# Attention scores in batches of four units instead of two, with the value products and output transposes of the loop in one PSUM bank

## The chip, the cores and the metric

The kernel runs on one core of a Trainium2 chip. The metric is the device time of one execution in microseconds (us). Of the kernel before there are three timed runs (median 454.51, from 453.69 to 454.97) and one profiled execution of 453.1 us, whose span from the first to the last instruction is 451.3 us.

## The reference

One encoder layer over 1024 tokens of width 1024. A combined projection makes queries, keys, values and gates of two groups of eight heads (head size 64). Group A attends within a window of 8 rows by 16 columns of the token grid (16 rows of 64) with a bias per head; group B attends within 128 tokens to either side, with two shared key/value heads, rotary positions and a sink logit. Both outputs are gated and concatenated, projected, added to the input and normalised:

```
h = x @ W_in
s = einsum('bqhd,biqjhd->bhqij', q_r, k_win) * scale + bias ; p = softmax(s)   # group A
s = where(valid, einsum('bnqkgd,bnjkd->bnkgqj', qb, k_band) * scale, -1e30)     # group B
p = softmax(concat([s, sink]))[..., :-1]
mixed = concat([y_a * silu(z_a), y_b * silu(z_b)])
x = layer_norm(alpha * x + mixed @ W_out, ln_gain, ln_bias)
```

## The kernel before, in words

Every product with a float32 operand is done as a sum of 16-bit ones: each operand is split into a high half and the rest, and high by high, high by rest and rest by high are added up in PSUM. For q times k the split halves of a query are stacked to 128 rows (64 of the high half, 64 of the rest): one product over 128 rows gives high by high plus rest by high at once (line 908), and a second one over 64 rows adds high by the rest of the key (line 912). The head `j` of a pair sets whether those 64 rows are the lower or the upper half of the array.

The work has four stages. Up to about 60 us: loading, scales and the value projection (lines 607 and 661). From 60 to 122 us: the first six column groups of the projection (line 404). From 122 to about 376 us: the attention loop, which also carries the other 15 column groups and the start of the output projection. After that: the rest of the output projection (line 1137) with the normalisation.

The attention loop has 128 units, each one head of one block of 128 queries; 64 of group B come first, then 64 of group A. A unit goes through these stages, each written at a fixed step `i` of the loop:

- `stage_mm` (lines 908 and 912) puts its scores into a PSUM bank of the tag `s`. Before, it is called at every even step for the units `i` and `i + 1`: two products over 128 rows, then two over 64 rows.
- `stage_qk` (line 937, VectorE): adds the bias or mask from the bank, writes `sn` and its minimum `nm`. Step `i`.
- `stage_exp` (line 952, ScalarE): the exponential of `sn`, written back into the unit's bank, with its sum. Step `i`.
- `stage_tr` (lines 962 on ScalarE, 963 on VectorE, 966 a transposing DMA of the SyncE queue): the high half and the rest of the probabilities, read from the bank, transposed into `tr`. Step `i + 1`. After line 963 the bank is free.
- `stage_pv` (line 992): for four units (a quad `q`) 30 or 36 small products of `tr` with the values, into a bank of the tag `t`. Step `4q + 9`.
- `stage_on` (line 1000, VectorE): divides by the sums. One step later.
- `stage_ot` (line 1010, four transposes, then line 1013 or 1019 on VectorE, which multiplies the gate `z`): before, for two quads at once, into another bank of the tag `t`, ahead of the value products of every second quad.

PSUM has eight banks of 128 x 512 float32: two for the projections (`pj`), four for scores (`s`) and two for all else (`t`), handed out in turn by `bank(tag)`; who takes a bank again waits for its last reader.

The order on each engine is the order in which the code is written. Between the stages `pump_to(u)` writes projection products ("fill") by a table: so many are due when the loop has reached step `u` (`FILL_N`, `FILL_AT`; 48 products for a column group, 24 to a half, about 24 for four units). The other engines' work for those groups is queued and taken out by `pop` at fixed places of a step. Once the loop has ended the order is that of the framework's scheduler (`final`).

Of the kernel before, what the change touches and what calls it, by code (L numbers as in the profile page):

```python
# [17 lines left out]
HD = 64  # L18
GW = 64
# [33 lines left out]
NPE = 384  # L53
PRE_AT = (12, 20)
WO_AT = [80, 84, 88, 92, 128, 129, 130, 131]
WO_LD = [18, 22, 26, 30, 36, 39, 42, 45, 48, 112, 116, 33, 130, 130]
# [10 lines left out]
def hybrid_block(ctx, tc, xT, x, wt, wv, wo, bias, sink, gain, lbias, cos, sin, bmask, out):  # L67
# [11 lines left out]
    def bank(tag):  # L79
        bufs = {"pj": 2, "s": 4, "t": 2}[tag]  # L80
        return (ps1 if bufs == 1 else ps2).tile([128, 512], F32, tag=tag, name=f"ps_{tag}", bufs=bufs)
# [162 lines left out]

    def w_scale(n):
# [190 lines left out]
    with ExitStack() as vctx:  # L436
# [139 lines left out]

        ROT = ("pj", "s", "t", "s")
        banks = {(t, a): bank(ROT[t]) for a in range(2) for t in range(4)}
        ordered.enter_context(tc.manual_schedule())
# [83 lines left out]

        set_a = [bank(r) for r in ROT]
        for i in range(3):
# [5 lines left out]
        for k in (0, 2):  # L671
            x2_lo(k)
        set_b = [bank(r) for r in ROT]
        for n, t in enumerate((2, 0, 1, 3)):
            for k in range(KT):
                for i in range(3):
                    v16(set_b[t], t, 1, k, i)
                if (n, k) == (0, 6):
                    w_scale(0)
                    w_split(0)  # L680
                    w_split(1)
                    x2_lo(4)
                    x2_lo(6)
                    x2_lo(7)
                if (n, k) == (1, 5):
                    w_scale(1)
# [44 lines left out]

        def z_sum(n):
            zps[n] = bank("t")
            nc.tensor.matmul(zps[n][:, :128], ones, cs[:, zabs[n] % 4], start=True, stop=True)
# [29 lines left out]
        def m_scale(i):  # L764
            n = NPRO + ZSUM[-1]
            if i == 0:
                z_sum(n)
# [205 lines left out]
    def stage_pv(q):  # L973
        ps = st[q, "o"] = bank("t")
        for m in range(4):
# [18 lines left out]
    def stage_on(q):  # L994
        ps = st.pop((q, "o"))
        ri = ap.tile([128, 4], F32, tag="ri", name="ri", bufs=4)
        nc.vector.reciprocal(ri, st.pop((q, "sm")))
        if q % 2 == 0:
            on[q // 2] = ap.tile([128, 2, 4, HD], F32, tag="on", name="on", bufs=2)
        nc.vector.tensor_mul(on[q // 2][:, q % 2], ps[:, :4 * HD].rearrange("p (m e) -> p m e", e=HD),  # L1000
                             ri.unsqueeze(2).to_broadcast([128, 4, HD]))

    def stage_ot(q):
        g, p, h = quad(q)
        h = h // 2
        need(*stk_ops.get(f"zb{p}" if g == "b" else f"z{p}", ()))
        ps = bank("t")
        o = on.pop(q // 2).rearrange("p q m e -> p (q m e)")
        for i in range(4):
            nc.tensor.transpose(ps[:, 128 * i:128 * i + 128], o[:, 128 * i:128 * i + 128], identf)  # L1010
        if g == "b":
            z = zt[4 + p][:, 512 * h:512 * h + 512]
            nc.vector.scalar_tensor_tensor(z, ps, z_col(4 + p), z, op0=ALU.mult, op1=ALU.mult)
        else:
            for i in range(2):
                b = 2 * h + i
                z = zt[p].rearrange("p (r c) -> p r c", c=GW)[:, :, 16 * b:16 * b + 16]
                src = ps[:, 256 * i:256 * i + 256].rearrange("p (r c) -> p r c", c=16)
                nc.vector.scalar_tensor_tensor(z, src, z_col(p), z, op0=ALU.mult, op1=ALU.mult)

# [33 lines left out]
    def wo_turn():  # L1054
        ps = bank("t")
        nc.tensor.transpose(ps[:, :128], wog.to_broadcast([128, 128]), identf)
# [97 lines left out]
    def final():  # L1154
# [96 lines left out]
        halves, normed = {}, [0]  # L1251
        for t, tag in ((0, "t"), (1, "t"), (2, "s")):
# [7 lines left out]
        tags = iter(("pj", "t", "pj", "t", "s", "s", "s", "s"))  # L1260
        for t, a in ((3, 1), (4, 1), (5, 0), (5, 1), (6, 0), (6, 1)):
# [18 lines left out]
    def gain_load():  # L1280
        gain_tile.append(zslot("gb"))
        nc.sync.dma_start(gain_tile[0], gain.partition_broadcast(128))

    clock["step"] = 0
    scan_ops = []
    for i in range(-LD, NU + LO):
# [33 lines left out]
        if i < NU:  # L1320
            if i % 2 == 0:
                us = units[i:i + 2]
                for u in us:
                    if u[3] in (0, 4):
                        need(*stk_ops[f"b{u[1]}", u[2], u[3] // 4])
                    if u[0] == "a" and i % 16 == 0:
                        need(*stk_ops[u[1], u[2], 0], *stk_ops[u[1], u[2], 1])
                stage_mm(us)
            stage_qk(units[i])
# [113 lines left out]
```

## Time and profile before

| | |
|---|---|
| three timed runs | 453.69, 454.51, 454.97 us |
| profiled execution, and its span | 453.1 us, 451.3 us |
| PE busy | 442.9 us (98%), 3271 products |
| weight loads (PEld) busy | 242.0 us (54%) |
| DVE (VectorE), ACT (ScalarE), POOL (GpSimd) busy | 344.9, 309.3, 219.0 us |
| line 404, projection products | 1008, 512 columns each |
| lines 908 and 912, score products | 128 each |
| TensorE clock granted | 0.997 of full speed |

A row of the timeline gives the start in us, the length in us, the engine, the line, the operation, `output<-inputs`, the shape and how many like instructions follow each other; in brackets the engine's idle time ahead of it and what ended it. Products overlap in the array, and the ends of products are modelled: how long one occupies the engine is read from the distance between two starts, not from its length. PEld is the load of the weights that stay in the array during a product. A row of a table by stretches gives start:end, the length, and for each engine its busy time and number of instructions, then the granted clock, the share of the DMA engines and GB/s.

### The profile page before, as it was taken

To read this page: it belongs to the slowest core of one execution; us is meant where nothing else is said; L and a number is where in the kernel's file an instruction comes from. 1 tells how busy PE (TensorE), PEld (TensorE's weight loads), DVE (VectorE), ACT (ScalarE), POOL (GpSimd) and SP (SyncE) were. 2 spreads that over 40 slices of the span, in tenths; PEclk is the share of its full clock that TensorE was granted. 3 is DMA by queue.
4 is the path that set the end of the run, shared out by engine and by line. 5 is a ranking of instruction groups with operands and counts; after the bars stand their busy time and mean duration, and the time that the engine had idled before them with its cause. 6 is when DMAs were issued, how large, how long until landed. Compare 5 with 4: busy or idle time off the path is not lost.

```text
span 451.3 us, 9483 instructions
## 1 busy us (share of the span) xinstructions
PE 442.9 (98%) x3271; PEld 242.0 (54%) x3271; DVE 344.9 (76%) x854; ACT 309.3 (69%) x718; POOL 219.0 (49%) x224
## 2 busy tenths in 40 slices
PE   9999999999999999999999999999999999999994
PEld 8996754444444455544545555555455554444442
DVE  5969958749988877777797888897776756379954
ACT  7679369767688988798978878887976876002211
POOL 0003934547838558658507528565662546005840
PEclk9999999999999999999999999999999999999998
DMA  8973088976847797597699799999999979101721
GB/s 297 378 254 93 14 284 260 303 275 241 253 130 155 130 191 143 124 147 158 130 176 200 166 166 195 198 223 175 204 209 178 168 139 371 52 0 62 248 87 70
DMA packets 133984, 81.76 MB, mean 181 GB/s; under 512 B 101296, under 2 KB 113328, under 8 KB 133680
## 3 DMA queue, kind: packets, MB, share of 16 engines
q1 hardware_dynamic: 133504, 80.67, 73.2%
q8 instruction: 25, 0.41, 0.4%
q10 hardware_dynamic: 432, 0.49, 0.3%
q14 instruction: 23, 0.19, 0.1%
HBM read 50.73 MB, written 9.96 MB: 134 GB/s over the span
## 4 chain that ended last, share of the span: by engine, by line
PE 68%; issue 9%; ACT 8%; POOL 7%; DVE 6%; DMA 1%; SPq 0%; POOLq 0%; DVEq 0%; ACTq 0%
PE ps_pj L404 26%; PE ps_s L1137 9%; PE ps_t L992 6%; PE ps_pj L1137 5%; PE ps_t L1137 5%; PE ps_s L908 3%; PE ps_s L661 3%; POOL wl L212 3%; PE ps_s L912 3%; PE ps_s L607 2%; POOL wr L211 2%; ACT ps_s L952 2%; DVE sn L937 2%; PE ps_t L661 1%; PE ps_pj L661 1%
## 5 line engine op out<-in xcount | busy, mean ns | idle before, releaser
L404 PE MATMUL ps_pj<-xf,wh 128*128 128x512 f16 x672 | 202.3, 380 | 0.0
L404 PE MATMUL ps_pj<-xf,wl 128*128 128x512 f16 x336 | 127.4, 379 | 0.0
L404 PEld LDWEIGHTS <-wh 128*128 128x128 f16 x672 | 60.2, 98 | 67.9 <-issue 6.1
L952 ACT ACTIVATE ps_s<-sn,nm 128x385 f32<-128x385 f32 (+3 forms) x128 | 70.0, 547 | 35.1 <-DVE nm L937 34.1
L963 DVE SCALAR_TENSOR_TENSOR split<-ps_s,split 128x384 f16<-128x384 f32 (+2 forms) x128 | 65.5, 512 | 20.3 <-ACT split L962 19.9
L1137 PEld LDWEIGHTS <-m 128*128 128x128 f16 x408 | 38.6, 98 | 42.6 <-issue 0.2
L962 ACT ACTIVATE split<-ps_s 128x384 f16<-128x384 f32 (+2 forms) x128 | 57.6, 450 | 2.4
L404 PEld LDWEIGHTS <-wl 128*128 128x128 f16 x336 | 32.9, 98 | 37.9 <-issue 0.7
L937 DVE CUSTOM_DVE_ANT_0 sn<-ps_s,bias,sg 128x264 f32<-128x264 f32 (+1 forms) x64 | 35.1, 549 | 17.4 <-PE ps_s L912 16.4
L937 DVE CUSTOM_DVE_ANT_0 sn<-ps_s,bm,nsk 128x384 f32<-128x384 f32 (+1 forms) x64 | 40.7, 635 | 4.6 <-PE ps_s L912 4.3
L211 POOL TENSOR_SCALAR wr<-wr,wsc 128x512 f32<-128x512 f32 x26 | 22.1, 848 | 43.0 <-ACT wh L206 36.8
L1137 PE MATMUL ps_s<-wo,m 128*128 128x512 f16 (+1 forms) x192 | 42.3, 372 | 0.0
L992 PEld LDWEIGHTS <-tr 128*128 128x128 f16 (+1 forms) x1104 | 36.6, 98 | 4.4
L884 POOL TENSOR_SCALAR bias<-bias,rsg 128x552 f32<-128x552 f32 (+1 forms) x24 | 18.9, 788 | 31.2 <-DMA bias<-in_bias 28.6
L212 POOL TENSOR_TENSOR wl<-wr,wh 128x512 f16<-128x512 f32 x26 | 31.6, 1215 | 2.2
L1194 ACT ACTIVATE sd<-mv,eps 128x1 f32<-128x1 f32 x8 | 2.4, 295 | 43.3 <-DVE mv L1192 41.0
L908 PE MATMUL ps_s<-ks,qs 128*128 128x384 f16 (+4 forms) x128 | 29.6, 306 | 1.5 <-DVE split L963 1.3
L1236 POOL TENSOR_TENSOR xr<-xr,gb 128x512 f32<-128x512 f32 x7 | 11.2, 1607 | 38.2 <-ACT xr L1233 38.2
L557 POOL TENSOR_SCALAR xraw<-xraw,xsc 128x512 f32<-128x512 f32 x3 | 5.5, 1825 | 40.1 <-ACT xf L552 40.1
L1137 PE MATMUL ps_pj<-wo,m 128*128 128x512 f16 (+1 forms) x120 | 24.9, 347 | 0.0
L952 ACT ACTIVATION_READ_ACCUMULATOR ps_s<-sn,nm 128x1 f32 x128 | 24.4, 191 | 0.2
L661 PEld LDWEIGHTS <-xf 128*128 128x128 f16 x192 | 18.3, 98 | 8.2 <-ACT xf L534 0.6
(208 smaller groups left out, 825.8 us busy)
## 6 DMA issues: line engine op xcount, KB each, us to landing
ws<-in_wt SPq DMA_DIRECT2D x15, 512.0 KB, 5.2
wr<-in_wt SPq DMA_DIRECT2D x26, 256.0 KB, 3.3
bias<-in_bias SPq DMA_DIRECT2D x16, 276.0 KB, 3.4
wor<-in_wo SPq DMA_DIRECT2D x16, 256.0 KB, 3.6
xr<-in_x SPq DMA_DIRECT2D x8, 512.0 KB, 8.7
xraw<-in_xT SPq DMA_DIRECT2D x15, 256.0 KB, 4.8
out<-xr SPq DMA_DIRECT2D x14, 256.0 KB, 2.0
bias<-in_bias SPq DMA_DIRECT2D x8, 368.0 KB, 3.9
```

The costliest lines, as they stand in the source:

```text
L211: nc.gpsimd.tensor_scalar(raw, raw, scale, 1.0, op0=ALU.mult, op1=ALU.mult)
L212: nc.gpsimd.tensor_sub(l, raw, h)
L404: nc.tensor.matmul(ps, a[:, k % 4, :], mv, start=(k == 0 and i == 0), stop=(k == KT - 1 and i == 2))
L661: nc.tensor.matmul(ps[:, :320], lh[1, k][:, 128 * t:128 * t + 128], rh[k][:, 320 * a:320 * a + 320], start=(k == 0 and i == 0), stop=(k == ...
L884: op = enq("pool", lambda: nc.gpsimd.tensor_scalar(bv, bv, rsg, -1.0, op0=ALU.mult, op1=ALU.mult), ld, prio=0)
L908: nc.tensor.matmul(ps[:, :m], q, sl[0], start=True, stop=False)
L937: nc.vector.tensor_tensor_reduce(sn[:, :m], ps[:, :m], bias_t, sg[:, c:c + 1], init, op0=ALU.add, op1=ALU.min, accum_out=nm)
L952: nc.scalar.activation(pt[:, :m], sn[:, :m], AF.Exp, bias=nm, scale=-1.0, accum_out=sm[:, k:k + 1])
L962: nc.scalar.activation(hl[:, :m, 0, :c], src, AF.Copy, scale=PSCALE)
L963: nc.vector.scalar_tensor_tensor(hl[:, :m, 1, :c], src, PSCALE, hl[:, :m, 0, :c], op0=ALU.mult, op1=ALU.subtract)
L992: nc.tensor.matmul(ps[:, o:o + HD], a, b_, start=(i == 0), stop=(i == len(mms) - 1))
L1137: nc.tensor.matmul(ps, lh[:, ts], rh[:, cs], start=(e == EO[0] and i == 0), stop=(e == EO[-1] and i == 2))
```

## The change

Scores are computed for four units at once. `batch(n)` collects what the units `n` to `n + 3` need and calls `stage_mm` with all four. It is called for the first four units ahead of the loop's first step, and then at every fourth step (`i % 4 == 3`) for the next four, after half of that step's fill. There are five banks `s` and one bank `t`. The third unit of each batch writes its probabilities into a tile `px` of SBUF instead of its bank, so that its bank is free after line 937. Value products use columns 0 to 255 of the one bank `t`, output transposes columns 256 to 511; transposes are done for each quad (two, not four at a time) after the value products of a later quad (`OT_AT`). `WARP` deals out the fill of four steps unevenly: 33, 21, 32 and 14%.

```diff
+WARP = (0, 0.33, 0.54, 0.86, 1)
+QK_AT = 0.5
-        bufs = {"pj": 2, "s": 4, "t": 2}[tag]
+        bufs = {"pj": 2, "s": 5, "t": 1}[tag]
...
+        if units.index(u) % 4 == 2:
+            pt = ap.tile([128, 388], F32, tag="px", name="px", bufs=1)
...
-        ps = st[q, "o"] = bank("t")
+        if q == 0:
+            st["t"] = bank("t")
+        ps = st["t"]
...
-        ps = bank("t")
-        o = on.pop(q // 2).rearrange("p q m e -> p (q m e)")
-        for i in range(4):
+        ps = st["t"][:, 0 if q == NU // 4 - 1 else 256:]
+        o = on.pop(q).rearrange("p m e -> p (m e)")
+        for i in range(2):
             nc.tensor.transpose(ps[:, 128 * i:128 * i + 128], o[:, 128 * i:128 * i + 128], identf)
...
     def pump_to(u):
         n = 0
+        k = int(u) % 4
+        u = int(u) // 4 * 4 + 4 * (WARP[k] + (WARP[k + 1] - WARP[k]) * (u - int(u)))
...
+    def batch(n):
+        us = units[n:n + 4]
+        for u in us:
+            if u[3] in (0, 4):
+                need(*stk_ops[f"b{u[1]}", u[2], u[3] // 4])
+            if u[0] == "a" and n % 16 == 0:
+                need(*stk_ops[u[1], u[2], 0], *stk_ops[u[1], u[2], 1])
+        stage_mm(us)
+
+    OT_AT = {(q, 0): (q - 3,) for q in range(3, 30)}
+    OT_AT.update({(29, 2): (27,), (30, 0): (28,), (31, 0): (29,), (32, 0): (30, 31)})
...
-            if i % 2 == 0:
-                us = units[i:i + 2]
...
-                stage_mm(us)
+            if i == 0:
+                batch(0)
             stage_qk(units[i])
...
-        if m == 0 and (3 <= q < NU // 4 and q % 2 == 1 or q == NU // 4):
-            stage_ot(q - 3 if q < NU // 4 else q - 2)
         if m == 0 and 0 <= q < NU // 4:
             stage_pv(q)
+        for k in OT_AT.pop((q, m), ()):
+            stage_ot(k)
...
         if i < NU:
             stage_exp(units[i])
+        if i % 4 == 3 and i + 1 < NU:
+            pump_to(i + QK_AT)
+            batch(i + 1)
```

Outside the loop the change only moves small sums and banks from the tag `t` to the tag `s`. In the output projection two of the banks that were `t` are `s`.

Where it shows in the order of the instructions, first on TensorE, at the scores of the first units of a column block of group A. Before, two units (`qs` the stacked queries, `ks` the stacked keys; line 404 is fill):

```order
L908 LDWEIGHTS qs
L908 MATMUL ps_s<-ks,qs 128x264
L908 LDWEIGHTS qs
L908 MATMUL ps_s<-ks,qs 128x288
L912 LDWEIGHTS qs
L912 MATMUL ps_s<-ks,qs 128x264
L912 LDWEIGHTS qs
L912 MATMUL ps_s<-ks,qs 128x288
L404 LDWEIGHTS wh_4128
L404 MATMUL ps_pj<-xf_538,wh_4128 128x512
```

After the change, at the same place (lines 908, 912 and 404 are now 910, 914 and 406):

```order
L910 MATMUL ps_s<-ks,qs 128x288
L914 LDWEIGHTS qs
L914 MATMUL ps_s<-ks,qs 128x264
L914 LDWEIGHTS qs
L914 MATMUL ps_s<-ks,qs 128x288
L914 LDWEIGHTS qs
L914 MATMUL ps_s<-ks,qs 128x264
L914 LDWEIGHTS qs
L914 MATMUL ps_s<-ks,qs 128x288
L406 LDWEIGHTS wh_4141
L406 MATMUL ps_pj<-xf_537,wh_4141 128x512
```

The row at the top is the last of four products over 128 rows; four products over 64 rows now follow each other before the fill goes on.

Second on VectorE, in a quad of group B for which the kernel before has no output transposes (`split` the halves of the probabilities, `z` the gate). Before:

```order
L937 ISA sn_1137,nm<-ps_s,bm,nsk,sg 128x384
L937 ISA nm 128x1
L963 SCALAR_TENSOR_TENSOR split_1132<-ps_s,split_1132 128x3x128
L286 SCALAR_TENSOR_TENSOR qs<-ps_pj,qs 64x512
L937 ISA sn_1136,nm<-ps_s,bm,nsk,sg 128x384
L937 ISA nm 128x1
L963 SCALAR_TENSOR_TENSOR split_1133<-ps_s,split_1133 128x3x128
```

After the change:

```order
L939 ISA sn_1137,nm<-ps_s,bm,nsk,sg 128x384
L939 ISA nm 128x1
L1017 SCALAR_TENSOR_TENSOR z_1858<-ps_t,zcol,z_1858 128x256
L967 SCALAR_TENSOR_TENSOR split_1132<-ps_s,split_1132 128x3x128
L288 SCALAR_TENSOR_TENSOR qs<-ps_pj,qs 64x512
L939 ISA sn_1136,nm<-ps_s,bm,nsk,sg 128x384
L939 ISA nm 128x1
L967 SCALAR_TENSOR_TENSOR split_1133<-ps_s,split_1133 128x3x128
```

The gate's product now stands in every quad, at half its width, between the scores of the quad's second unit and the splits of its first and second unit. Apart from these rows VectorE has the same order as before, and ScalarE too but for one swap of neighbours.

Third on TensorE, at the end of the loop, the last output transposes. Before:

```order
L1010 MATMUL ps_t<-identf,on 128x128 x2
L1137 LDWEIGHTS m_4732
L1137 MATMUL ps_t<-wo_5443,m_4732 128x512
L1137 LDWEIGHTS m_4732
L1137 MATMUL ps_t<-wo_5443,m_4732 128x512
```

After the change:

```order
L1014 MATMUL ps_t<-identf,on 128x128 x4
L1141 LDWEIGHTS m_4747
L1141 MATMUL ps_t<-wo_5456,m_4747 128x512
L1141 LDWEIGHTS m_4747
L1141 MATMUL ps_t<-wo_5456,m_4747 128x512
```

Before, the last four transposes stand in two pairs with five products of the output projection between them, and 24 products into `t` banks follow that need nothing of the loop; now all four stand together and 12 such products follow.

More of the change, by code (lines that the diff above doesn't have):

```diff
@@ L243, in z_tree, with w_scale @@
             nc.vector.tensor_add(cs[:, zabs[n] % 4], a[:, 0], a[:, 1])
-    def w_scale(n):
+    def w_scale(n, tag="s"):
         g, v = wg[:, n:n + 1], inv[:, n:n + 1]
         c, m = (2 * n, 2) if n < NPRO else (2 * NPRO, NS)
-        ps = bank("t")
+        ps = bank(tag)
         if n in ZPRO:
@@ L575, in v_max @@
             nc.vector.tensor_reduce(vm[:, t:t + 1], v32[t], axis=AXX, op=ALU.max, apply_absolute_value=True)
-        ROT = ("pj", "s", "t", "s")
-        banks = {(t, a): bank(ROT[t]) for a in range(2) for t in range(4)}
+        ROT = ("pj", "s", "t", "s"), ("pj", "s", "s", "s")
+        banks = {(t, a): bank(ROT[a][t]) for a in range(2) for t in range(4)}
         ordered.enter_context(tc.manual_schedule())
@@ L662, in v16 @@
                              start=(k == 0 and i == 0), stop=(k == KT - 1 and i == (2 if a == 0 else 2)))
-        set_a = [bank(r) for r in ROT]
+        set_a = [bank(r) for r in ROT[0]]
         for i in range(3):
@@ L672, in hybrid_block @@
             x2_lo(k)
-        set_b = [bank(r) for r in ROT]
+        set_b = [bank(r) for r in ROT[1]]
         for n, t in enumerate((2, 0, 1, 3)):
@@ L678, in hybrid_block @@
                 if (n, k) == (0, 6):
-                    w_scale(0)
+                    w_scale(0, "t")
                     w_split(0)
@@ L685, in hybrid_block @@
                 if (n, k) == (1, 5):
-                    w_scale(1)
+                    w_scale(1, "t")
                     nc.vector.tensor_scalar_mul(nsk, sk, -1.0)
@@ L730, in hybrid_block, with z_sum @@
         zps = {}
-        def z_sum(n):
-            zps[n] = bank("t")
+        def z_sum(n, tag="s"):
+            zps[n] = bank(tag)
             nc.tensor.matmul(zps[n][:, :128], ones, cs[:, zabs[n] % 4], start=True, stop=True)
@@ L766, in m_scale @@
             if i == 0:
-                z_sum(n)
+                z_sum(n, "t")
             elif i == 1:
@@ L994, in stage_on @@
     def stage_on(q):
-        ps = st.pop((q, "o"))
+        ps = st["t"]
         ri = ap.tile([128, 4], F32, tag="ri", name="ri", bufs=4)
         nc.vector.reciprocal(ri, st.pop((q, "sm")))
-        if q % 2 == 0:
-            on[q // 2] = ap.tile([128, 2, 4, HD], F32, tag="on", name="on", bufs=2)
-        nc.vector.tensor_mul(on[q // 2][:, q % 2], ps[:, :4 * HD].rearrange("p (m e) -> p m e", e=HD),
+        on[q] = ap.tile([128, 4, HD], F32, tag="on", name="on", bufs=4)
+        nc.vector.tensor_mul(on[q], ps[:, :4 * HD].rearrange("p (m e) -> p m e", e=HD),
                              ri.unsqueeze(2).to_broadcast([128, 4, HD]))
@@ L1004, in stage_ot @@
         g, p, h = quad(q)
-        h = h // 2
         need(*stk_ops.get(f"zb{p}" if g == "b" else f"z{p}", ()))
-        ps = bank("t")
-        o = on.pop(q // 2).rearrange("p q m e -> p (q m e)")
-        for i in range(4):
+        ps = st["t"][:, 0 if q == NU // 4 - 1 else 256:]
+        o = on.pop(q).rearrange("p m e -> p (m e)")
+        for i in range(2):
             nc.tensor.transpose(ps[:, 128 * i:128 * i + 128], o[:, 128 * i:128 * i + 128], identf)
         if g == "b":
-            z = zt[4 + p][:, 512 * h:512 * h + 512]
-            nc.vector.scalar_tensor_tensor(z, ps, z_col(4 + p), z, op0=ALU.mult, op1=ALU.mult)
-        else:
[L1015 to L1019, printed above, removed]
+            z = zt[4 + p][:, 256 * h:256 * h + 256]
+            nc.vector.scalar_tensor_tensor(z, ps[:, :256], z_col(4 + p), z, op0=ALU.mult, op1=ALU.mult)
+        else:
+            z = zt[p].rearrange("p (r c) -> p r c", c=GW)[:, :, 16 * h:16 * h + 16]
+            src = ps[:, :256].rearrange("p (r c) -> p r c", c=16)
+            nc.vector.scalar_tensor_tensor(z, src, z_col(p), z, op0=ALU.mult, op1=ALU.mult)
     for b in range(4):
@@ L1054, in wo_turn @@
     def wo_turn():
-        ps = bank("t")
+        ps = st["t"][:, 256:]
         nc.tensor.transpose(ps[:, :128], wog.to_broadcast([128, 128]), identf)
@@ L1251, in final @@
         halves, normed = {}, [0]
-        for t, tag in ((0, "t"), (1, "t"), (2, "s")):
+        for t, tag in ((0, "t"), (1, "s"), (2, "s")):
             obank[t, 1] = bank(tag)
@@ L1259, in final @@
                     finish(t, a, obank[t, a])
-        tags = iter(("pj", "t", "pj", "t", "s", "s", "s", "s"))
+        tags = iter(("pj", "t", "pj", "s", "s", "s", "s", "s"))
         for t, a in ((3, 1), (4, 1), (5, 0), (5, 1), (6, 0), (6, 1)):
@@ L1320, in hybrid_block @@
         if i < NU:
-            if i % 2 == 0:
-                us = units[i:i + 2]
[L1323 to L1327, printed above, removed]
-                stage_mm(us)
+            if i == 0:
+                batch(0)
             stage_qk(units[i])
```

## The prediction, made before the changed kernel was run

> **What bounds the kernel now.** I read the busy shares first, then the waits of TensorE (PE), then the attention loop as a table by stretches, then single batches in the timeline. The page:
>
> ```profile
> PE 442.9 (98%) x3271; PEld 242.0 (54%) x3271; DVE 344.9 (76%) x854; ACT 309.3 (69%) x718; POOL 219.0 (49%) x224
> PEclk9999999999999999999999999999999999999998
> ```
>
> PE is busy for 442.9 of 451.3 us at full granted clock; no other engine comes near. These are all the waits of PE that the view of waits names inside the program:
>
> ```profile
> PE ps_t L1219 <- ACT dg L1218: 1.5, 1, 1.5
> PE ps_s L908 <- DVE split L963: 1.3, 2, 0.7
> PE ps_t L444 <- DVE warm L441: 1.0, 1, 1.0
> ```
>
> Of 451.3 us some 4 are waits, and only the 1.3 us at line 908 lie in the loop. So time can be won only in what PE itself spends on its instructions, and lost wherever another engine becomes late. The loop in four stretches (PE, PEld, DVE, ACT, POOL):
>
> ```profile
> 122.00:151.00 29.00, 27.99 (x195) 12.76 (x192) 24.66 (x75) 24.49 (x61) 18.25 (x17) 1.00 0.63 146
> 151.00:177.00 26.00, 26.00 (x240) 13.61 (x240) 19.39 (x58) 22.46 (x59) 15.05 (x15) 1.00 0.87 171
> 177.00:213.00 36.00, 35.59 (x303) 18.09 (x300) 27.81 (x78) 30.02 (x80) 26.18 (x26) 1.00 0.73 137
> 213.00:372.00 159.00, 158.88 (x1470) 84.29 (x1470) 124.29 (x354) 128.98 (x326) 80.11 (x94) 1.00 0.96 180
> ```
>
> From 151 us on PE has no gap but 0.5 us in 221. In the first 29 us it stands idle for 1.0 us, and there DVE (24.66 of 29) sets the pace. PE's wait for a bank there,
>
> ```profile
> 143.37 0.55 DVE L963 SCALAR_TENSOR_TENSOR split<-ps_s,split 128x384 f16<-128x384 f32 x1
> 143.96 0.32 PE L908 MATMUL ps_s<-ks,qs 128*128 128x384 f16 x1 [0.73 <-DVE split L963]
> ```
>
> ends when line 963 has read the bank. Now what a batch costs PE. Starts are what to read:
>
> ```profile
> 188.85 0.38 PE L404 MATMUL ps_pj<-xf,wl 128*128 128x512 f16 x1
> 189.06 0.49 PE L908 MATMUL ps_s<-ks,qs 128*128 128x384 f16 x2
> 189.49 0.34 PE L912 MATMUL ps_s<-ks,qs 64*128 64x384 f16 x2
> 189.75 0.60 PE L404 MATMUL ps_pj<-xf,wh 128*128 128x512 f16 x2
> ```
> ```profile
> 304.60 1.21 PE L992 MATMUL ps_t<-va,tr 128*128 128x64 f16 x36
> 305.65 0.60 PE L404 MATMUL ps_pj<-xf,wh 128*128 128x512 f16 x2
> 306.95 0.40 PE L908 MATMUL ps_s<-ks,qs 128*128 128x264 f16 x2
> 307.28 0.30 PE L912 MATMUL ps_s<-ks,qs 64*128 64x264 f16 x2
> 307.50 0.61 PE L404 MATMUL ps_pj<-xf,wh 128*128 128x512 f16 x2
> ...
> 308.16 0.59 PE L404 MATMUL ps_pj<-xf,wh 128*128 128x512 f16 x2
> ...
> 309.46 0.59 PE L404 MATMUL ps_pj<-xf,wh 128*128 128x512 f16 x2
> ```
>
> Six fill products start between 308.16 and 309.46: 1.30 / 6 = 0.217 us for 512 columns. At that rate 384 columns are 0.163 us. The first batch occupies 189.75 - 189.06 = 0.69 us. Two products over 128 rows make 0.33; if the two over 64 rows, which sit in opposite halves of the array, run side by side, they make 0.16. That leaves 0.69 - 0.49 = **0.20 us** unexplained. The second batch (264 and 288 columns, by the order of the instructions) occupies 307.50 - 306.95 = 0.55, and by columns 0.112 + 0.122 + 0.122 = 0.36: **0.19 to 0.20 us** again. What doesn't grow with the columns belongs to going into the 64-row form and out of it, once each in a batch. I take 0.205, which starts given to 0.01 us allow.
>
> **The change part by part.**
>
> *Fewer batches.* 64 batches become 32; the products are the same. 32 goings in and out fall away: 32 x 0.205 = 6.6 us at most. The four batches lost to the pace of DVE must be taken off: up to about 151 us (the first 16 units, four batches of four) DVE's chain decides, and a shorter PE only waits longer. 28 x 0.205 = **5.7 us**.
>
> Does a batch of four have a cost that two don't? The row of its loads:
>
> ```profile
> L912 PEld LDWEIGHTS <-qs 64*128 64x128 f16 x128 | 6.1, 92 | 20.1 <-issue 20.1
> L404 PEld LDWEIGHTS <-wh 128*128 128x128 f16 x672 | 60.2, 98 | 67.9 <-issue 6.1
> L992 PEld LDWEIGHTS <-tr 128*128 128x128 f16 (+1 forms) x1104 | 36.6, 98 | 4.4
> ```
>
> The third 64-row product loads into the half in which the first still runs. Lower bound: nothing, as at line 404, where 672 loads of 98 ns over the whole array disappear behind products of 0.217 us; they reload exactly the rows in use. Even the 36 value products of 64 columns above take 305.65 - 304.60 = 1.05 us, 29 ns each, with a load of 98 ns for each. No gain below nothing: products already start at the rate of their columns. Upper bound for an exposed load: 0.095 x 32 = 3.0 us; and if the second pair doesn't run side by side at all, 0.16 x 28 = 4.5 us. I take nothing, the nearest rows.
>
> The Trainium skill speaks against this change here: "TensorE: Matmul & The Clock Gate", section "Part 3: Packing small matmuls — row/col tiling", says that loads overlap products in flight only when their row groups differ. By it the second pair's loads would be exposed, and the sum would lose the 3.0 us. The rows of lines 404 and 992 disagree, at least for the full array; no trace of before has two pairs in a row.
>
> *The hand-over from the paced stretch.* By the order of the instructions PE has done one fill product less (0.22 us) where DVE releases it, and it waits there with its third rather than its second product over 128 rows (0.16): **-0.4 us**. Bounds: 0 and -0.7, the longest wait shown at line 908.
>
> *Output transposes* are as many as before, 64, two at a time, now right behind value products. Before, the pairs that interrupt other work show what one costs:
>
> ```profile
> 374.96 0.38 PE L1010 MATMUL ps_t<-identf,on 128*128 128x128 f32 x2
> 375.18 1.24 PE L1137 MATMUL ps_s<-wo,m 128*128 128x512 f16 x5
> 376.25 0.38 PE L1010 MATMUL ps_t<-identf,on 128*128 128x128 f32 x2
> 376.47 5.34 PE L1137 MATMUL ps_t<-wo,m 128*128 128x512 f16 x24
> 381.65 0.59 PE L1137 MATMUL ps_pj<-wo,m 128*128 128x512 f16 x2
> ```
>
> 375.18 - 374.96 = 0.22 for two, 0.11 each, without a price for going in or out: nothing on PE. On VectorE eight instructions of 512 columns become sixteen of 256:
>
> ```profile
> L1019 DVE SCALAR_TENSOR_TENSOR z<-ps_t,zcol,z 128x256 f32<-128x256 f32 x16 | 7.0, 477 | 6.7 <-PE ps_t L1010 6.7
> L1013 DVE SCALAR_TENSOR_TENSOR z<-ps_t,zcol,z 128x512 f32<-128x512 f32 x8 | 6.0, 747 | 0.0
> ```
>
> 16 x 0.477 - 6.0 = 1.6 us more of DVE, in group B, where DVE is near its limit only up to 151 and from 177 to 213 us. It lies beside PE; uncovered it costs 0.2 us at each of eight places. Value products that share their bank with transposes: the `on` of the quad before has been read a whole quad (7.6 us) earlier, so no wait, at most a start.
>
> *Waits for banks.* A batch of four with five banks waits for line 963 of the units 0 and 1 of the batch before and for line 937 of its unit 2. This wait is new in its place; behind it on PE stands everything, fill too. Its price is the ring below, nothing by my count. What falls away in exchange is DVE's waiting for line 912:
>
> ```profile
> DVE sn L937 <- PE ps_s L912: 20.6, 24, 1.6
> ```
>
> This is DVE's slack, not PE's, and worth nothing by itself.
>
> *The end of the loop.* Before, the last two transposes (376.25) are followed by 24 products that need nothing of them; then come the products that need the last `m` and `wo`:
>
> ```profile
> 377.48 1.41 DVE L1047 TENSOR_TENSOR m<-z,m 128x512 f16<-128x512 f32 x1
> 378.81 1.64 DVE L1099 TENSOR_TENSOR wo<-wor,wo 128x512 f16<-128x512 f32 x1
> 380.38 1.64 DVE L1047 TENSOR_TENSOR m<-z,m 128x512 f16<-128x512 f32 x1
> ```
>
> The low half of `wo` is ready at about 380.4, 4.2 us after the transposes. After the change 12 independent products and seven of high halves stand ahead of its first reader: 19 x 0.217 = 4.1 us. A wait of **0.2 us**; bounds 0 and 1.5 (a further DVE instruction late).
>
> **Sum** for the profiled execution: 453.1 - (5.7 - 0.4 - 0.2) = 453.1 - 5.1 = 448.0. It ran 1.4 below the median of the timed runs; the median becomes 454.5 - 5.1, with the rounded terms carried out **449.3 us**.
>
> **The rivals.**
>
> *The ring turns into the bound* (slower). From a batch's first 64-row product the release goes: out of the form and nine fill products 0.27 + 1.95, value products 1.05, two transposes 0.22 and their end 0.16: 3.65 on PE. Then DVE in its order: `z` 0.48, split of unit 0 0.55, one queued instruction, line 937 of unit 2, its split of unit 1:
>
> ```profile
> L286 DVE SCALAR_TENSOR_TENSOR qs<-ps_pj,qs 64x512 f16<-64x512 f32 x16 | 11.0, 688 | 1.4 <-ACT qs L280 0.9
> L937 DVE CUSTOM_DVE_ANT_0 sn<-ps_s,bm,nsk 128x384 f32<-128x384 f32 x48 | 32.1, 669 | 4.5 <-PE ps_s L912 4.3
> L937 DVE DVE_READ_ACCUMULATOR2_ANT nm<- 128x1 f32 x128 | 10.5, 82 | 0.0
> L963 DVE SCALAR_TENSOR_TENSOR split<-ps_s,split 128x384 f16<-128x384 f32 x80 | 44.3, 554 | 13.7 <-ACT split L962 13.5
> ```
>
> 0.69 + 0.67 + 0.08 + 0.55: together 6.67, and from the third 128-row product to the next 64-row one 0.42: 7.1 us. PE's own work for four units is 24 x 0.217 + 1.05 + 0.22 + 1.19 = 7.7, against 7.9 before. So 0.6 us of slack. It decides against the change if the ring passes 7.9: a second queued DVE instruction (0.69) and one late ACT do that. At 8.0 each of 28 rounds loses 0.15: +4 us, **458.5**. For it: the stretch 177 to 213 us, where ACT is busy 30.0 of 36. Against: 213 to 372 us, DVE 78%, ACT 81%.
>
> *Exposed loads*: 5.1 - 3.0 = 2.1 us gained, **452.2**.
>
> *DVE and ACT pace more of the loop* than the first 16 units, ten batches more (up to 213 us): 10 x 0.205 = 2.1 less, 3.0 gained, **451.5**.
>
> *The second pair runs one after the other*: 5.1 - 4.5 = 0.6, **453.9**, the same.
>
> **How the numbers follow.** Forecast 0.62; exposed loads 0.12; paced 0.07; pairs in sequence 0.07; ring 0.12. A measurement here tells 0.3% (1.4 us) from no change: faster 0.62 + 0.12 + 0.07 = 0.81, same 0.07, slower 0.12. Low end: all 32 batches (6.6) and half of the 1.3 us at line 908: 454.5 - 7.3 = 447.2. High end: exposed loads, and the 0.6 by which runs of one kernel differ: 454.5 - 2.1 + 0.6 = 453.0. Left out: 0.19.
>
> **What would show each step.** Right: 32 batches of about 1.19 us with 384 columns, from the first 128-row product to the next fill; the waits of PE at the 128-row line below 2 us after 151 us; DVE's 20.6 us at line 937 gone; the same unit reached about 0.2 us earlier with each four units from 151 us on. Wrong: batches of 1.28 (loads) or 1.35 (sequence); a wait of PE for line 967 (963 before) in each round (ring), named at the third or fourth product; a gap before the first low-half product after the loop.

## The result, and the profile after

The changed kernel takes 456.9 us (median of 13 runs, 454.7 to 458.7), the kernel before 454.09 us in its 13 runs beside them (453.5 to 455.31): a ratio of 1.0064, 95% interval 1.0048 to 1.008. Forecast was 449.3, so it is slower where it should have been faster. The profiled execution took 456.78 us, its span 455.1 us, 3.8 more than before.

The head of the page:

```profile
PE 441.0 (97%) x3271; PEld 243.1 (53%) x3271; DVE 351.2 (77%) x862; ACT 310.8 (68%) x718; POOL 221.2 (49%) x224
PEclk9999999999999999999999999999999999999999
```

PE is busy for 1.9 us less and idle for more. What it waits for inside the loop and at its end (view of waits: total us, times, longest):

```profile
PE ps_s L910 <- DVE nm L939: 3.8, 3, 2.0
...
PE ps_t L1014 <- DVE on L1005: 0.7, 1, 0.7
PE ps_t L1060 <- DVE on L1005: 0.7, 1, 0.7
PE ps_t L1014 <- DVE z L1021: 0.6, 1, 0.6
PE ps_t L1141 <- DVE eps L1162: 0.6, 1, 0.6
PE ps_s L910 <- DVE split L967: 0.4, 2, 0.2
```

Before, one row of 1.3 us stood for the loop. Now there are six, of 6.8 us, and four of them name the single bank `t`. By stretches, in the columns of the table before:

```profile
122.00:151.00 29.00, 26.18 (x165) 11.45 (x163) 25.38 (x70) 23.26 (x56) 17.34 (x17) 0.94 0.57 137
151.00:177.00 26.00, 26.00 (x237) 13.61 (x232) 21.72 (x59) 22.23 (x58) 14.77 (x14) 1.00 0.81 149
177.00:213.00 36.00, 35.91 (x330) 19.13 (x330) 29.45 (x80) 31.12 (x82) 26.93 (x27) 1.00 0.81 144
213.00:372.00 159.00, 155.90 (x1440) 83.72 (x1439) 128.56 (x360) 131.53 (x330) 84.40 (x96) 1.00 0.99 183
```

The first stretch has lost 30 of 195 products, and its granted clock is 0.94 where it was 1.00. An undisturbed batch looks as forecast:

```profile
161.39 0.81 PE L910 MATMUL ps_s<-ks,qs 128*128 128x384 f16 x4
162.13 0.50 PE L914 MATMUL ps_s<-ks,qs 64*128 64x384 f16 x4
162.56 0.39 PE L406 MATMUL ps_pj<-xf,wh 128*128 128x512 f16 x1
```

162.56 - 161.39 = 1.17 us for four units, 0.20 above the rate of the columns. So it is in 25 of the 32 batches. The other seven are longer, by waits. The longest:

```profile
143.43 0.49 PE L910 MATMUL ps_s<-ks,qs 128*128 128x384 f16 x2
145.90 0.27 PE L910 MATMUL ps_s<-ks,qs 128*128 128x256 f16 x1 [1.98 <-DVE nm L939]
146.37 0.35 PE L910 MATMUL ps_s<-ks,qs 128*128 128x256 f16 x1 [0.20 <-DVE split L967]
146.65 0.71 PE L914 MATMUL ps_s<-ks,qs 64*128 64x384 f16 x4
147.30 0.61 PE L406 MATMUL ps_pj<-xf,wh 128*128 128x512 f16 x1
147.70 0.63 PE L406 MATMUL ps_pj<-xf,wl 128*128 128x512 f16 x1
148.13 1.06 PE L406 MATMUL ps_pj<-xf,wh 128*128 128x512 f16 x2
148.98 0.63 PE L406 MATMUL ps_pj<-xf,wl 128*128 128x512 f16 x1
```

The third product stands 2 us for the bank of unit 10, until line 939 has read it. And behind the wait 512 columns take 148.98 - 148.13 = 0.85 for two, 0.43 each: twice 0.217. The granted clock, in the trace, is 0.5 from 146.43 to 149.85 us and 1.0 on either side.

What px does to VectorE's split: groups by shape, then two single ones, the second beside GpSimd:

```profile
L967 DVE SCALAR_TENSOR_TENSOR split<-ps_s,split 128x384 f16<-128x384 f32 x60 | 33.1, 552 | 7.6 <-ACT split L966 7.2
L967 DVE SCALAR_TENSOR_TENSOR split<-px,split 128x384 f16<-128x384 f32 x20 | 16.2, 810 | 2.6 <-ACT split L966 2.5
```
```profile
232.94 0.55 DVE L967 SCALAR_TENSOR_TENSOR split<-px,split 128x384 f16<-128x384 f32 x1
```
```profile
200.91 1.27 POOL L338 TENSOR_TENSOR rp_raw<-rp_raw,cos 128x512 f32<-128x512 f32 x1 [3.91 <-DVE rp_sw L337]
201.25 1.35 DVE L967 SCALAR_TENSOR_TENSOR split<-px,split 128x384 f16<-128x384 f32 x1
...
202.14 1.59 POOL L339 TENSOR_TENSOR rp_sw<-rp_sw,sin 128x512 f32<-128x512 f32 x1
```

From a bank the split takes 0.552 us, from px 0.810 on average: 0.55 where GpSimd rests, up to 1.35 where it works. The rows above show how: the GpSimd instruction that was running ends at 200.91 + 1.27 = 202.18, the split at 201.25 + 1.35 = 202.60, 0.42 later. Of the 20 splits of 384 columns from px, 14 began while a GpSimd instruction was at work, and each ended 0.40 to 0.42 us after it; the other six took 0.55 us. So the split waits until the running GpSimd instruction is over. It isn't the only one with both inputs in SBUF. A product of one column, before the change and after it, each with GpSimd's instruction:

```profile
136.54 1.27 POOL L337 TENSOR_TENSOR rp_sw<-rp_sw,sin 128x512 f32<-128x512 f32 x1
137.59 0.24 DVE L778 TENSOR_TENSOR zg<-zg,vg 128x1 f32<-128x1 f32 x1
```
```profile
138.95 1.47 POOL L340 TENSOR_TENSOR rp_raw<-rp_raw,rp_sw 128x512 f32<-128x512 f32 x1
139.21 1.22 DVE L780 TENSOR_TENSOR zg<-zg,vg 128x1 f32<-128x1 f32 x1
```

Both end with GpSimd (137.83 and 137.81; 140.43 and 140.42). The longer split ahead of it has moved the one column to the start of a GpSimd instruction, and 0.24 us became 1.22. The end of the loop:

```profile
376.23 4.70 PE L1141 MATMUL ps_s<-wo,m 128*128 128x512 f16 x21
380.77 0.38 PE L1014 MATMUL ps_t<-identf,on 128*128 128x128 f32 x2
381.73 0.44 PE L1014 MATMUL ps_t<-identf,on 128*128 128x128 f32 x2 [0.58 <-DVE z L1021]
382.74 0.59 PE L1141 MATMUL ps_t<-wo,m 128*128 128x512 f16 x2 [0.57 <-DVE eps L1162]
```

The second pair of transposes waits for VectorE's read of the first, and the first output product into the bank for VectorE's read of the second (the row names line 1162, a small write that VectorE does just behind that read).

**Where the 3.7 us went.** Each product is charged with the distance to the next start; what exceeds the rate of the columns is sorted by cause (profiled executions, us, worked out from the starts of all products):

| | before | after | difference | forecast |
|---|---|---|---|---|
| into the 64-row form and out, 0.205 each | 13.1 | 6.6 | -6.6 | -5.7 |
| waits for banks at the score products, with 0.4 of half clock in the batch at 143 us | 2.4 | 6.7 | +4.3 | +0.4 |
| transposes of the loop | 7.0 | 8.1 | +1.1 | 0 |
| fill above its rate (half clock) | 0 | 0.9 | +0.9 | 0 |
| waits for bank `t`: line 1060 | 0 | 0.84 | +0.8 | 0 |
| waits for bank `t`: quad 27, and the two at the end | 0 | 0.86, 0.74, 0.74 | +2.3 | +0.2 |
| ahead of the loop | | | +0.8 | 0 |
| sum | | | +3.6 | -5.1 |

The ends differ by 3.7.

### The profile page after: what moved, and what is told of

Read it like the earlier page. It is cut to its first block, busy times and chain, and to the rows that moved or that the text cites. A ratio compares the mean times of both kernels' runs of the same rounds, so it can differ in the third digit from the quotient of the medians.

```text
span 455.1 us, 9455 instructions
## 1 busy us (share of the span) xinstructions
PE 441.0 (97%) x3271; PEld 243.1 (53%) x3271; DVE 351.2 (77%) x862; ACT 310.8 (68%) x718; POOL 221.2 (49%) x224
## 4 chain that ended last, share of the span: by engine, by line
PE 60%; issue 10%; DVE 9%; ACT 8%; POOL 7%; DMA 5%; SPq 0%; ACTq 0%; POOLq 0%; DVEq 0%
PE ps_pj L406 25%; PE ps_s L1141 11%; PE ps_t L998 6%; PE ps_pj L1141 4%; PE ps_s L663 4%; PE ps_s L910 3%; POOL wl L214 3%; DVE split L967 2%; PE ps_t L1141 2%; DVE sn L939 2%; PE ps_s L914 2%; POOL wr L213 2%; ACT ps_s L956 2%; PE ps_t L1014 2%; DMA wos<-in_wo 1%
## 5 line engine op out<-in xcount | busy, mean ns | idle before, releaser
L406 PE MATMUL ps_pj<-xf,wh 128*128 128x512 f16 x672 | 207.8, 381 | 0.0
L406 PEld LDWEIGHTS <-wh 128*128 128x128 f16 x672 | 65.2, 98 | 77.7 <-issue 8.3
L956 ACT ACTIVATE ps_s<-sn,nm 128x385 f32<-128x385 f32 (+3 forms) x96 | 52.4, 546 | 20.7 <-DVE nm L939 20.1
L967 DVE SCALAR_TENSOR_TENSOR split<-ps_s,split 128x384 f16<-128x384 f32 (+2 forms) x96 | 49.0, 511 | 9.8 <-ACT split L966 9.1
L1141 PE MATMUL ps_s<-wo,m 128*128 128x512 f16 (+1 forms) x240 | 52.3, 374 | 0.0
L966 ACT ACTIVATE split<-ps_s 128x384 f16<-128x384 f32 (+2 forms) x96 | 43.3, 451 | 1.9
L910 PE MATMUL ps_s<-ks,qs 128*128 128x384 f16 (+4 forms) x128 | 25.3, 307 | 4.6 <-DVE nm L939 3.8
L967 DVE SCALAR_TENSOR_TENSOR split<-px,split 128x384 f16<-128x384 f32 (+2 forms) x32 | 23.6, 737 | 3.1 <-ACT split L966 2.8
L956 ACT ACTIVATE px<-sn,nm 128x385 f32<-128x385 f32 (+3 forms) x32 | 18.6, 582 | 10.7 <-DVE nm L939 9.7
```

What stands on the lines that cost most here:

```text
L406: nc.tensor.matmul(ps, a[:, k % 4, :], mv, start=(k == 0 and i == 0), stop=(k == KT - 1 and i == 2))
L910: nc.tensor.matmul(ps[:, :m], q, sl[0], start=True, stop=False)
L956: nc.scalar.activation(pt[:, :m], sn[:, :m], AF.Exp, bias=nm, scale=-1.0, accum_out=sm[:, k:k + 1])
L966: nc.scalar.activation(hl[:, :m, 0, :c], src, AF.Copy, scale=PSCALE)
L967: nc.vector.scalar_tensor_tensor(hl[:, :m, 1, :c], src, PSCALE, hl[:, :m, 0, :c], op0=ALU.mult, op1=ALU.subtract)
L1141: nc.tensor.matmul(ps, lh[:, ts], rh[:, cs], start=(e == EO[0] and i == 0), stop=(e == EO[-1] and i == 2))
```

## The experiments

Three theories, which can hold together. A: px, which lies in SBUF, lengthens VectorE's chain where that sets the pace. B: the ring of banks (a batch of four in five banks) makes PE wait. C: the single bank `t` makes PE wait. Beside them: did the merge of the batches win what was forecast? Times are medians; the kernel before took 453.77 to 454.05 us beside these runs.

### px alone, in the kernel before

```diff
         pt = st.pop((u, "ps"))
+        if units.index(u) % 4 == 2:
+            pt = ap.tile([128, 388], F32, tag="px", name="px", bufs=1)
```

> The kernel before, with one part of the change alone: the third unit of each four writes its probabilities into the SBUF tile px, in place of its bank. Theory A (the split that reads px on VectorE is slowed while GpSimd works, so VectorE's chain grows where it sets the pace): the splits from px take 0.7 to 0.8 us on average where those from a bank take 0.51, VectorE's busy time grows by 6 to 7 us, its chain over units 4 to 16 by about 2 us, and the whole is 1.5 to 2.5 us slower than before, near 456. Theory B (the waits come from the ring of banks) and theory C (they come from the single bank t): no more than 0.5 us from before.

454.66 us, ratio 1.0018 (1.0007 to 1.003): slower by 0.6 to 0.8 us, less than A said. The split from px took 0.813 us:

```profile
L965 DVE SCALAR_TENSOR_TENSOR split<-ps_s,split 128x384 f16<-128x384 f32 x60 | 33.2, 554 | 9.4 <-ACT split L964 9.3
L965 DVE SCALAR_TENSOR_TENSOR split<-px,split 128x384 f16<-128x384 f32 x20 | 16.3, 813 | 2.9 <-ACT split L964 2.9
```

VectorE's way from unit 4 to unit 16 grew from 20.9 to 23.1 us, as much as in the changed kernel. So px alone makes that chain longer by 2.2 us, the product of one column included (1.22 us here too); PE's waits at the scores grew by only 1.2 us (1.3 to 2.5).

### Without px, in the changed kernel

```diff
-        if units.index(u) % 4 == 2:
-            pt = ap.tile([128, 388], F32, tag="px", name="px", bufs=1)
```

> The changed kernel without px: the third unit keeps its bank until its split has been read. Theory A: every split takes 0.51 us on average, VectorE's first 16 units take some 2 us less, and if nothing else is touched the time falls by about 2 us to 455. Theory B: the fourth product of a batch now waits for a split that stands 0.7 to 1.3 us later in VectorE's order, with a slack of 0.6 us at most, so 0.1 to 0.5 us are lost in each of 31 batches: 459 to 465. Theory C: as the changed kernel, within 0.5 us.

477.8 us, ratio 1.0524 (1.0507 to 1.0542). All three theories missed; B's direction is right and its size far too small. One row of the waits:

```profile
PE ps_s L910 <- DVE split L965: 20.3, 22, 2.1
```

A batch of four in five banks needs px: else PE waits for a split 22 times, 0.92 us each. Little or nothing can be left there of the slack that I took for 0.6 us.

### The old order inside a batch

```diff
-        stage_mm(us)
+        stage_mm(us[:2])
+        stage_mm(us[2:])
```

> The changed kernel with the products of a batch in the old order, twice two over 128 rows and two over 64 rows; place, banks, px and fill stay. If merging won what the starts showed (0.2 us for each going in and out): PE's sum over the score products grows by 6.1 us, of which the waits of the first 16 units swallow 0.8 to 1.5, so 461 to 462.5. If the merge won nothing (loads of the second pair exposed, or products not side by side): the time of the changed kernel, 456.9, within 0.7.

460.39 us, 3.5 more than the changed kernel and under the 461 to 462.5 expected. In the profiled execution (461.61, 4.8 more) PE's sum over the score products without the waits grew by 5.6 us, and its waits in the loop shrank by 1.9. An undisturbed batch costs 0.42 us above its columns, twice the 0.21 of the changed kernel. The merge did its work; a part of what it wins turns into waiting.

### The end of the loop

```diff
-(31, 0): (29,), (32, 0): (30, 31)
+(31, 0): (29,), (31, 2): (30,), (31, 3): (31,)
```

> The changed kernel with the last two pairs of output transposes two steps and one step earlier and apart (quad 30, then three fill products, then quad 31), so that the second pair doesn't stand behind the first one's read by VectorE. Theory C (single bank t at the end costs 2.3 us in three waits of 0.86, 0.74 and 0.74): the middle one goes, 0.7 to 1.0 us less than the changed kernel, near 456.0. Theories A and B alone: no change, within 0.4.

455.97 us (455.85 to 456.2), 0.9 less. The wait of 0.74 between the transposes is gone, that of 0.74 behind them has stayed. C holds for this place.

### Batches of two in the stretch that VectorE paces, without and with px

```diff
+            if i % 2 == 0 and i < 16:
+                batch(i, 2)
-        if i % 4 == 3 and i + 1 < NU:
+        if i % 4 == 3 and 15 <= i and i + 1 < NU:
```

(`batch` takes the number of units as a second argument here.) The first of the two runs also has `and units.index(u) >= 16` in the condition of px.

> The changed kernel with batches of two and no px for the first 16 units, where VectorE sets the pace; from unit 16 on as changed. Theory A (px in reach of GpSimd lengthens VectorE's chain there): units 4 to 16 take 20.9 us of VectorE's time axis, as in the kernel before, in place of 23.1, the wait of 2.3 us at the scores of units 12 to 15 goes, and the time falls by about 2.2 us to 454.7. Theory B (the ring of four in five banks alone): the same fall, since the ring is gone there too; the next run tells them apart.

457.9 us, where 454.7 was expected. VectorE's way over units 4 to 12 is again that of the kernel before (14.5 us), so px was what lengthened it, and not the ring. Up to unit 16, which the first batch of four brings, it is 21.8 us and not the 20.9 expected. And the time didn't fall: the first batch of four, for units 16 to 19, now waits 2.8 us at 150 us. PE has its work done early in either case and stands until VectorE has caught up; the wait only moves.

> The same batches of two for the first 16 units, but with px for their third units. Theory A: units 4 to 16 take 23.1 us as in the changed kernel, and the time stays within 0.6 us of 456.9. Theory B: 20.9 us and 454.7, as without px.

456.77 us, VectorE's units 4 to 16 in 23.1 us: as A said, and not B. But since the run without px was no faster, neither px nor the ring in the first 16 units is by itself what the time hangs on: the waits come at the next place either way (here 1.9 us at 151 us).

### The batch behind all the fill of its step

```diff
-QK_AT = 0.5
+QK_AT = 1
```

> The changed kernel with each batch behind all the fill of its step and not behind half of it: some two fill products or 0.4 us more for the ring of banks. If the waits for banks come at many batches by small amounts (theory B), 31 times a part of 0.4 us is won: 2 us or more, under 455. If they stand at three places only (136, 143 and 214 us, theory A and VectorE's queue), at most 0.4 us each: 455.7 to 457.3.

454.86 us, 2.0 less than the changed kernel: B's number. Its waits, though, stand at two places (136 and 213 us), as A said, and sum to 4.4 us in the starts where they were 5.4. Which share is the ring and which VectorE's queue this run can't tell: units 4 to 12 take 15.3 us, 16.3 in the changed kernel, but units 4 to 16 take the same 23.1.

### All mends of the first look together

The edits of the run without px in the first 16 units and of the end of the loop, and the transposition for the output scale one step earlier:

```diff
-        if i == WO_MAX + 3:
+        if i == WO_MAX + 2:
             wo_turn()
-        if WO_MAX + 4 <= i < WO_MAX + 7:
-            wo_scale(i - WO_MAX - 4)
+        if WO_MAX + 3 <= i < WO_MAX + 6:
+            wo_scale(i - WO_MAX - 3)
```

> All mends together: batches of two without px for the first 16 units, the last output transposes apart, and the transposition for the output scale one step earlier, ahead of the read by VectorE that it waited 0.84 us for. If the three losses add up: 456.9 - 2.2 - 0.9 - 0.8 = 453.0, some 1.1 us under the kernel before (454.1). If the waits only move on to the next place: 454 to 455.

456.05 us (453.59 to 458.73), above both expectations: 1.9 less than the run with batches of two and no px (457.9), of which 1.6 are the waits of 0.84 and 0.74 that went, but from the wrong base. The waits of the early stretch moved, as in that run.

### The late batch with the two mends

> The changed kernel with the three mends that each took away a wait: batch behind all the fill of its step (454.9 alone), last output transposes apart (0.9 less), transposition for the output scale a step earlier (its wait of 0.84 us gone in the run before). If they add: 454.9 - 0.9 - 0.8 = 453.2, at or just under the kernel before (453.8 to 454.1). If a mended wait comes back elsewhere: 454 to 455.

The edits are `QK_AT = 1`, that of the end of the loop and that of the output scale. 453.98 us, ratio 1.0001 (0.9987 to 1.0015): 0.9 us of the expected 1.7, now even with the kernel before.

### More fill in the early stretch

```diff
-FILL_AT = [0, 8, 17, 25, 33, 
+FILL_AT = [0, 7, 15, 24, 32.5, 
```

> The run above with more fill in the first 16 units: the first two column groups due at steps 7 and 15, not 8 and 17, so that some ten products more are done where PE waits for VectorE at 136 to 150 us. Theory A and half clock (a wait of over 2 us is followed by some seven products at 0.427 us): the wait of 2.5 us shrinks under 1, the slow products go, 2 to 3.5 us less than the run above, about 450.5. Rival (VectorE gets the column groups' own work earlier and its chain grows by as much): no gain, 452.7 to 454.

454.56 us, 0.6 more than without. The wait at 136 us fell from 2.3 to 1.0 and no product of the loop ran at half clock, but new waits of 1.1 came at 145, of 1.3 at 153 and of 1.8 at 182 us. The rival was right: VectorE gets the column groups' own work earlier, and its way over units 4 to 16 grew from 23.0 to 25.2 us.

> The same with half the advance (steps 7.5 and 16). Theory A and half clock: the wait falls to 1 to 1.5 us, short enough that no slow products follow (waits of up to 1.26 us had none in the kernel before and with px alone): 1.5 to 2.5 us less than without, about 451.3. Rival: no gain.

455.46 us, 1.5 more than without (steps 7.5, 16 and 24.5): no gain either. The wait at 136 us is still 2.3 us, yet no product of the loop ran at half clock.

> The kernel before with the same advance of fill as in the run with steps 7 and 15. It waits 0.9 us for its banks in this stretch and never runs at half clock, so at most 0.9 us are to be won: 453.2 to 454.1. If the early fill were worth as much here as in the changed kernel (2 us or more), what is won there would have nothing to do with the batches.

453.65 us, ratio 0.9987 (0.9973 to 1.0001): no difference that can be told.

### Quad 27 ahead of the other read of its bank

```diff
-(29, 2): (27,), (30, 0): (28,)
+(29, 1): (27,), (30, 0): (28,)
```

> The run with the three mends (late batch, last output transposes apart, output scale earlier), and the transposes of quad 27 written ahead of VectorE's read of quad 29 in the same bank and not behind it. Theory C (the waits come from the one bank, read by VectorE at other columns): the wait of 0.86 us at 361 us goes, 0.8 us less: 453.2. If the wait belongs to quad 27's own data: no change, 454.0.

**452.52 us**, ratio 0.9976 (0.9965 to 0.9987) to the kernel before: 1.5 less than its twin, and faster than both kernels. The wait of 0.86 us is gone (of the rest, 0.5 us lies ahead of the loop in the two profiled executions, where nothing was edited, and so isn't shown to come from the edit), although nothing of quad 27's own data changed: PE was held by VectorE's read of quad 29, in other columns of the same bank.

### PE kept busy with useless products

18 products of 256 columns that nobody reads, ahead of the batch for units 8 to 11:

```diff
+        if n == 8:
+            m, q, sl = qk_parts(us[0])
+            for _ in range(18):
+                nc.tensor.matmul(st["t"][:, 256:], q, sl[0][:, :256], start=True, stop=True)
         stage_mm(us)
...
+        if i == 7:
+            st["t"] = bank("t")
```

(The bank `t` is taken earlier, so that these products can write it.)

> The run above with 18 products that nobody reads (256 columns, some 1.95 us, into the free columns of bank t) right ahead of the batch for the units 8 to 11, where PE else waits 2.0 to 2.3 us. Theory half clock (the idleness lowers PE's clock for some 3 us): the wait falls to 0.3 us, no product of 0.427 us follows, and the kernel is 1.0 to 1.5 us faster than its twin although it does more work: 451.9. Rival (the slow products come from the batch or from VectorE's lateness): they stay, and the time is that of the twin or 0.3 us more.

452.79 us. Its twin's wait and the 3 us behind it, then the same places here (the granted clock is the third number from the end of a row):

```profile
135.50:139.40 3.90, 1.92 (x9) 0.42 (x7) 3.82 (x10) 1.78 (x5) 3.82 (x4) 0.87 0.74 157
139.40:142.40 3.00, 3.00 (x20) 1.30 (x19) 2.93 (x11) 2.67 (x8) 0.33 (x1) 0.60 0.66 131
```
```profile
136.26:140.00 3.74, 3.50 (x28) 2.21 (x27) 3.67 (x9) 1.66 (x4) 3.66 (x4) 1.00 0.70 174
140.00:143.00 3.00, 3.00 (x42) 1.82 (x41) 2.92 (x12) 2.61 (x8) 0.71 (x1) 1.00 0.56 111
```

Idle, PE has a granted clock of 0.60 behind the wait and starts 20 products in 3 us; kept busy, it has 1.00 and starts 42. So it is the idleness that lowers the clock, as expected; the time, 0.9 us above the expected 451.9, is that of the twin all the same: VectorE is in front here, and what PE wins it waits at the next two batches (0.8 and 0.3 us).

## Why the prediction was wrong

- *What bounds the kernel*: right before the change, in all but the first 29 us.
- *Fewer batches*: right, in mechanism and size. 0.205 us for each batch saved, in 25 batches undisturbed, and paid again in the run with the old order; the loads of the second pair aren't exposed. The rule of the Trainium skill ("TensorE: Matmul & The Clock Gate", section "Part 3: Packing small matmuls — row/col tiling") that was weighed there didn't show: 1.17 us for a batch, and not 1.28.
- *Waits for banks*, "nothing by my count": **the step that failed**. They cost 4.3 us more (0.4 was forecast, for the hand-over). The ring was added up from durations of one quiet stretch, with each instruction of VectorE starting at once; a late one (line 939 behind 1.7 us of other work at 143 us, behind line 367, for which VectorE waits 1.6 us, at 214 us) stops all of PE, since the fill stands behind the waiting product. The rival "the ring turns into the bound" had the right place of the wait and the wrong pattern: not 0.15 us in each round, but 0.9, 2.5 and 2.0 us at 136, 143 and 214 us. (Exposed loads, priced there at 452.2, come to 452.4 by their own terms: 454.5 - 2.1.) VectorE ahead of the two long waits, which end with line 939:

```profile
143.45 1.19 DVE L787 TENSOR_TENSOR zcol<-vscb,msc 128x1 f32<-128x1 f32 x2
144.57 0.71 DVE L337 STREAM_SHUFFLE rp_sw<-rp_raw 128x512 f32<-128x512 f32 x1
145.19 0.65 DVE L939 CUSTOM_DVE_ANT_0 sn<-ps_s,bm,nsk 128x384 f32<-128x384 f32 x1
...
214.87 0.69 DVE L367 SCALAR_TENSOR_TENSOR z<-z,ps_pj 128x512 f32<-128x512 f32 x1 [1.60 <-ACT z L366]
215.48 0.54 DVE L939 CUSTOM_DVE_ANT_0 sn<-ps_s,bm,nsk 128x256 f32<-128x256 f32 x1
```

- *px was not priced at all.* I counted the instructions of VectorE and not where their operands lie. The runs with px alone, and with and without it in batches of two, show px to be the cause of the 2.2 us by which VectorE's chain of the early stretch grew. About 1 us of that is the product of one column, which px only moved. How much of PE's waiting at 136 and 143 us is px and how much the ring stays open, because the ring doesn't run without px. At 214 us it is not px by itself: there px alone leaves PE's wait at 0.56 us, with 0.53 in the kernel before and 1.44 in the changed one. The Trainium skill has the rule, "VectorE: DVE Perf Modes", section "Two Vector instructions with no wait between them": with two SBUF inputs VectorE reads one through an interface shared with GpSimd. The trace agrees: 0.55 us alone, up to 1.35 beside GpSimd.
- *Output transposes*, "nothing on PE": mis-sized. Right behind value products a pair takes 0.25 us and not 0.22 (340.07 to 340.32); 32 pairs, 1.1 us.

```profile
339.02 1.21 PE L998 MATMUL ps_t<-va,tr 128*128 128x64 f16 x36
340.07 0.42 PE L1014 MATMUL ps_t<-identf,on 128*128 128x128 f32 x2
340.32 0.38 PE L406 MATMUL ps_pj<-xf,wh 128*128 128x512 f16 x1
```

- *The end of the loop*, 0.2 us: mis-sized and for the wrong reason. The 12 products I called independent write the bank that VectorE still reads. With quad 27 and line 1060, bank `t` costs 3.2 us.
- *Ahead of the loop*: 0.8 us that no step spoke of. The first products ran at half clock for longer (320 columns in 0.27 us and not 0.15, up to 6.3 us). It differs from run to run with no edit there: by its records in the trace the granted clock is first full at 3.9 us with px alone, at 4.6 in the kernel before, at 6.5 in the changed one and at 10.2 without px. Whether the change has a part in it stays open.

## What to carry to other kernels

When PE is the bound and a change gives it less work, ask first how far each engine beside it is from its own limit, stage by stage: what PE wins where another engine paces only lengthens a wait. Fewer banks in turn show as a few long waits at single late instructions, and two readers and writers of one bank hold each other even at different columns; where the data allow it, write PE's product ahead of VectorE's read. Price an edit by where operands lie as well as by what it computes.

## What the runs showed of the hardware

- Each spell of half clock in the loop lasted 3.41 us in every trace (0.427 us for 512 columns), and began a whole number of 3.41 us after the moment at which the clock had first become full (in the changed kernel at 6.49 + 41 x 3.413 = 146.43 us). What goes with it is how long PE stood idle within the 3.41 us just before. Over all 16 traces, from 100 to 440 us and by the idle times of the timeline, idleness of 1.9 us or more in one such stretch was followed by half clock all 11 times, 1.4 to 1.7 us three times of eight, 1.35 us and less never. Where the stretches begin differs from trace to trace (the clock first becomes full between 3.8 and 10.2 us), so the same wait can cost or not: without px a wait of 1.75 us at 150 us, with 0.36 just ahead, put 1.89 us into one stretch and was followed by half clock; one of 1.73 us at 134 us was cut into 0.83 and 0.90 and was not. In the changed kernel the wait of 2.5 us at 143 us so cost 1.3 us more. The Trainium skill ("TensorE: Matmul & The Clock Gate", section "Part 1: The HAM clock gate (the "warmup" mystery)") gives half rate after an idle window of about 3.4 us; here the stretch has that length, but 1.9 us of idleness in it was enough, and at times 1.4.
- VectorE's split with both operands in SBUF takes up to 2.5 times as long while GpSimd works (0.55 to 1.35 us); from a PSUM bank it stays at 0.55. It doesn't slow evenly. In all traces 168 splits of 384 columns from px began while a GpSimd instruction had been running for 0.1 us or more, with at least 0.15 us to go: every one ended 0.40 to 0.42 us after that instruction. Even one column takes 1.22 us in place of 0.24 when it starts early in a GpSimd instruction.
